# Attention's values by seven block products for eight, in a two-layer decoder trunk on one Trainium2 core

## The chip, the cores and the metric

The kernel runs on one core of one Trainium2 chip. The metric is the device time of one execution in microseconds. The engines of the core are named as in the profile: PE (TensorE), DVE (VectorE), ACT (ScalarE), POOL (GpSimd) and SP (SyncE, which issues most loads).

## The reference

256 tokens of width 2048 go through two layers in float32. Layer 0 has a recurrent mixer, layer 1 has attention; each is followed by an MLP of width 8192.

```python
for layer in range(DEPTH):
    hn = rms_norm(h, norm_mix[layer])
    if layer % 2 == 0:
        mix = recurrent_mixers(hn, ...)
    else:
        mix = dilated_attention(hn, positions, w_qkv[j], w_o[j])
    h = h + mix
    h = h + squared_relu_mlp(rms_norm(h, norm_mlp[layer]), mlp_w1[layer], mlp_w2[layer])
return rms_norm(h, final_norm)

def dilated_attention(h, positions, w_qkv, w_o):
    qkv = (h @ w_qkv).reshape(bsz, seq, 3, ATTN_HEADS, HEAD_DIM)
    q = partial_rope(qkv[:, :, 0], positions) * (HEAD_DIM ** -0.5)
    k = partial_rope(qkv[:, :, 1], positions)
    v = qkv[:, :, 2]
    ...   # softmax over keys inside three dilated windows, merged by their denominators
    return out @ w_o
```

Attention has 16 heads of 128 features; `w_qkv` is 2048 x 6144.

## The kernel before, in words

**Products in float32.** A weight matrix comes from memory in units of 128 x 2048 numbers (1 MB). ACT rounds each to a high part (`hi`, L102), DVE subtracts to get the low part (`lo`, L103); activations are kept split in the same way (`bufa`, `bufb`). A product is three matmuls: high x high, high x low, low x high (`mm`, L181). Units pass through three buffers each of `raw`, `hi` and `lo`; SP issues the loads in one planned order (`units`, `fetch`), and a load waits for its buffer.

**Block products.** The MLP works on pairs of 512 output columns (`blocks`). Of the eight block products of a 2 x 2 by 2 x 2 block matrix over half of the depth, seven do: the units `a`, `t1`, `t2`, `c`, `t3`, `d`, `t4` are single blocks or sums of blocks of the weights, made by DVE (`combine`, L130) and by accumulating loads on POOL (L142, L148). Each is multiplied with one of the sums of activation blocks in `formx` (or `formh`), 12 matmuls of 128x512. The other half of the depth is multiplied plainly: four units `n`, 24 matmuls each. `ORDERS` holds the order of the products. The results pass between PSUM banks by copies (`hold`) and sums (`final`, `u3`). `formx` is filled from the residual's features by `combos` (L597 to L600) and `part_forms` (L593, L594).

**From tokens to features.** After a residual block is complete (`to_x`, L754, or `add_res`, L609), PE transposes it (`turn`, L184), and ACT and DVE write it split into `bufa` (`split_to`, L235, L236). These turns (`to_features`) stand in a list `later`, which `flush` works off after certain products. At the end of the first MLP the blocks come in the order 1, 0, 3, 2; none of them goes to `formx` there.

**Attention.** Values come in four groups of 512 columns (`tokens_group`), each by plain products: 4 units, 96 matmuls of 128x512. A head takes two projections (`project`: 16 matmuls of 128x512 and 16 of 128x256 each), scaling (L421 to L423), the rotary rotation (`rope`, L853 to L856), the score products (L866, L867), mask, maximum, exponential and division (L869 to L877), three transposes (L880), and the product with the values (`mix`, L888, L889), which is split into `bufb` (L232, L233). The order is: values of heads 0 to 3, those heads, values of 4 to 7, those heads, values of 8 to 11, those heads, heads 12 to 15 up to their weights, their values, their mixes. The rotary tables (`rotary`) are asked for behind the first group of values. Then comes the output projection (`out_project`), whose products go through `bufb` in four groups of four heads for each of four column blocks.

A planner fixes the order of instructions on each engine before the run; PE's product matmuls are chained in program order (`chain`), while score products, transposes of scores and mixes are put between them by the planner. `urgent` raises a priority.

Of the kernel before, what the change touches and what calls it, by code (L numbers as in the profile page):

```python
# [20 lines left out]
P = 128  # L21
# [20 lines left out]
def trunk_kernel(ctx, tc, x, xtok, cols, tab, masks, pos, fin, w_in, w_gate, w_out, w_qkv, w_o, w1, w2, out):  # L42
# [81 lines left out]
    def combine(u, src, i, what, i0):  # L124
        def load(name, j, home=wraw):
            held[name] = home.tile([P, 2048], F32, name="raw" if home is wraw else name)
            nc.sync.dma_start(held[name], src[j])

        def add(to, x, y):
            V.tensor_tensor(held[to], held[x], held[y], OP.add)  # L130

        if what == "a":
            load("t1", i0 + 4, pair)
            load("a", i)
            held["s"] = pair.tile([P, 2048], F32, name="s")
# [8 lines left out]
        if ahead == ("t4",) and src not in T4_DMA(w1, w2):  # L144
            add("s", "s", "d")
        made[u] = Weights(held[{"t1": "s", "t2": "s", "t3": "t1", "t4": "s"}.get(what, what)])
        if what == "c" and src in T4_DMA(w1, w2):
            nc.gpsimd.dma_start(held["s"], src[i0 + 1], accum_op=OP.add)  # L148
# [155 lines left out]
    def over_tokens(r):  # L304
        p = psc.tile([P, 512], F32, name="pt", bufs=1)
        for j in range(2):
            T.transpose(p[:, j * P:j * P + P], r[:, j:j + 1].to_broadcast([P, P]), ident)
        return p[:, :S]
# [15 lines left out]
    def tokens(src, i0, mov, kgs=(0, 1, 2, 3), by_k=False):  # L324
        ks = PAIRED if src is w2 else range(KB)
        ps = [pmm.tile([P, 512], F32, name="p") for _ in range(2)]
        for g in kgs:
            w = unit(src, i0 + g)
            order = [(j, i) for i in range(4) for j in range(2)] if by_k else \
                [(j, i) for j in range(2) for i in range(4)]  # L330
            for j, i in order:
                k = ks[4 * g + i]
                h, l = w.part(i * 512, 512)
                xh = mov[:, k, j * P:j * P + P]
                xl = mov[:, k, S + j * P:S + j * P + P]
                first, last = g == kgs[0] and i == 0, g == kgs[-1] and i == 3
                mm(ps[j], xh, h, start=first, stop=False)
                mm(ps[j], xh, l, start=False, stop=False)
                mm(ps[j], xl, h, start=False, stop=last)
            flush()  # L340
        return ps
# [9 lines left out]
    def project(src, i, mov, acc=None):  # L351
        w = unit(src, i)
        p = pmm.tile([P, 512], F32, name="p")
        jobs = [(k, mov[:, k], k == 0, k == KB - 1) for k in range(KB)]
        if later:
            cross(p, w, jobs[:8], "h")
            flush()
            cross(p, w, jobs[8:12], "h")
            cross(p, w, jobs[:12], "l")
            jobs = jobs[12:]  # L360
        (acc or cross)(p, w, jobs)
        return p
# [224 lines left out]
    def open_pairs(layer):  # L587
        pool_ = pairs.enter_context(tc.tile_pool(name=f"pair{layer}", bufs=1))
        return pool_, [pool_.tile([P, 4, 2, 512], F32R, name=n) for n in ("formx", "formh")]
# [12 lines left out]
    pair, (formx, formh) = open_pairs(0)  # L602
# [11 lines left out]
    def to_features(n, gname, forms=None):  # L614
        def work():
            with urgent():
                for half in range(2):
                    p = psc.tile([P, 2, S], F32, name="pl", bufs=2)
                    for j in range(2):
                        for i in range(2):  # L620
                            k = 4 * n + 2 * half + i
                            turn(p[:, i, j * P:j * P + P], xres[:, j, k * P:k * P + P])
                    k = 4 * n + 2 * half
                    if forms is None:
                        for i in range(2):
                            split_to(bufa[:, k + i], p[:, i], col(gname, k + i))
                        continue
                    z = pair.tile([P, 2, 2, P], F32, name="y21")
                    for i in range(2):
                        A.activation(z[:, i], p[:, i].rearrange("p (j c) -> p j c", j=2), AF.Copy,  # L630
                                     scale=col(gname, k + i))
                    zs = z.rearrange("p i j c -> p i (j c)")
                    split_to(bufa[:, k:k + 2], zs)
                    a11, a21, a12, a22 = (z[:, i, j] for i in range(2) for j in range(2))
                    combos(a22, a11, a21, a12, a11, a21, a12, a22)
                    part_forms(forms, k // 2, 1, slice(0, 4), z.rearrange("p i j (one c) -> p one (i j) c", one=1))
        later.append(work)
# [10 lines left out]
    def blocks(src, i0, n0, mov, forms, events, final, soon=False):  # L648
# [6 lines left out]
        beta = psc.tile([P, 512], F32, name="po" if n0 else "pd", bufs=1)  # L655
# [14 lines left out]
        for what, u in ORDERS[src is w2]:  # L670
            w = unit(src, None if u is None else i0 + 4 * n0 + u)
            if what != "n":
# [3 lines left out]
                if what == "t1" and soon:  # L676
                    flush()
                continue
            n, g = divmod(u, 4)
            plains[n] += 1  # L680
            due = len(later)
            for j in (1, 0) if n else (0, 1):
                times(sums[n, j], w, lambda i, j=j, g=g: plain(j, 4 * g + i))
                if plains[n] == 2:
                    final(n, j, sums[n, j])
            flush(due)
# [24 lines left out]
    def first(i0, n0, soon):  # L711
# [23 lines left out]
        def final(n, j, bank):  # L735
            with urgent():
# [5 lines left out]
                else:  # L742
# [5 lines left out]
                                             "t3": u3}, final, soon)  # L748
# [24 lines left out]
    def mlp(layer, nrm, nxt, gname):  # L773
# [13 lines left out]
        for q in range(4):  # L787
            ends = nxt if q == 3 else None

            def done(n):  # L790
                if ends is None:
                    return
                if gname:
                    to_features(n, gname)
# [6 lines left out]
            for n in (0, 2):  # L801
                first(layer * 64 + q * 16, n, q + n == 0)
# [8 lines left out]
    vgs = mixers.enter_context(tc.tile_pool(name="vgs1", bufs=2))  # L811
    wk = mixers.enter_context(tc.tile_pool(name="wk2", bufs=2))
    rot = mixers.enter_context(tc.tile_pool(name="rot", bufs=1))
# [3 lines left out]
    def rotary():  # L817
        ppi = rot.tile([32, S], I32, name="ppi")
        nc.gpsimd.dma_start(ppi, bass.AP(tensor=pos.tensor, offset=pos.offset, ap=[[0, 32], [1, S]]))
        ang = rot.tile([32, S], F32, name="ang")  # L820
        cosT = rot.tile([32, S], F32, name="cosT")
        sinT = rot.tile([32, S], F32, name="sinT")
        V.tensor_copy(ang, ppi)
# [22 lines left out]
    rt = rstd(nx1)  # L846
    rs = tmp.tile([P, S], F32, name="nr", bufs=1)
    A.copy(rs, over_tokens(rt))
# [9 lines left out]
    def scores(u0):  # L858
# [9 lines left out]
        s = wk.tile([P, 384], F32, name="as", bufs=3)  # L868
# [12 lines left out]
        st = wk.tile([P, 384], F32, name="pT", bufs=5)  # L881
# [3 lines left out]
    def mix(hd, st, vg, bank="po", bufs=1):  # L885
        vs = slice((hd % 4) * P, (hd % 4) * P + P)
# [5 lines left out]
    pend = []  # L892
    for g in range(4):
        if g < 3:
            vg = tokens_group(w_qkv, g * 12, rt, kgs=(0, 1, 2, 3) if g else (0, 1, 3, 2))
        if not g:
            rotary()
        for hd in range(4 * g, 4 * g + 4):
            u0 = g * 12 + (4 if g < 3 else 0) + (hd % 4) * 2
            st = scores(u0)  # L900
            if g < 3:
                mix(hd, st, vg)
            else:
                pend.append(st)
    vg = tokens_group(w_qkv, 44, rt)
    for hd, bank in zip(range(12, 16), (("po", 1), ("pd", 1), ("pl", 2), ("pl", 2))):
        mix(hd, pend[hd - 12], vg, *bank)

    mixers.close()
    pair, (formx, formh) = open_pairs(1)  # L910
# [54 lines left out]
T4_DMA = lambda w1, w2: (w1,)  # L965
# [32 lines left out]
def _layout(a):  # L998
# [30 lines left out]
    q_, k_, v_ = feat(wq[:, :2048]), feat(wq[:, 2048:4096]), toks(wq[:, 4096:])  # L1029
    w_qkv = []  # L1030
    for g in range(4):
        if g < 3:
            w_qkv.append(v_[4 * g:4 * g + 4])
        for h in range(4 * g, 4 * g + 4):
            w_qkv += [q_[h:h + 1], k_[h:h + 1]]
    w_qkv.append(v_[12:])
# [33 lines left out]
```

## Time and profile before

| | |
|---|---|
| median of 3 runs | 2166.9 us (2166.84 to 2166.93) |
| the profiled execution's own time | 2166.9 us |
| its span, first to last instruction | 2165.1 us |
| granted PE clock | 0.998 |
| busy PE, DVE, ACT, POOL | 2146.9, 1792.2, 1254.1, 44.7 us |
| first MLP's last quarter | about 931 to 1101 us |
| attention up to the output projection | 1100.7 to 1391.1 us |

A row of groups gives line, engine, operation, output and inputs, shapes and count; then busy time, mean duration in ns, and idle time of the engine before them with what ended it. A row of the timeline gives start, duration, engine, line, and in brackets the idle time before it. A row of stretches gives length, then busy time (and count) of PE, PE's weight loads, DVE, ACT and POOL, then clock, share and rate of the loads. Durations of matmuls are longer than their spacing, since they are pipelined.

### The profile page before, as it was taken

The numbers are of one execution on the slowest core, as the hardware profiler recorded it, in microseconds if no ns is written. First come the engines' busy times: TensorE is split into PE (matmuls) and PEld (weight loads), VectorE is DVE, ScalarE is ACT, GpSimd is POOL, SyncE is SP. The second block draws the span as 40 slices with busy tenths as digits, with TensorE's granted clock in tenths as the row PEclk, the third lists the DMA queues.
The fourth block names the chain that finished last, engine by engine and source line by source line (L and its number), as shares of the span: only waits on it lengthen the run. The fifth ranks groups of instructions, "written<-read, shape, count | busy, mean of one in ns | idle before, by whom it ended". The sixth has DMA issues, their size and how long they took to land.

```text
span 2165.1 us, 27716 instructions
## 1 busy us (share of the span) xinstructions
PE 2146.9 (99%) x11044; PEld 1833.8 (85%) x11044; DVE 1792.2 (83%) x2094; ACT 1254.1 (58%) x1413; POOL 44.7 (2%) x57
## 2 busy tenths in 40 slices
PE   9999999999999999999999999999999999999997
PEld 8999998888888888888788888888888888888886
DVE  7776787789889889889877768667998998898897
ACT  7444485566466566466554544456655755755764
POOL 0000000000000000000000000000000000000000
PEclk9999999999999999999999999999999999999999
DMA  8444445587777687687664554557768777777873
GB/s 319 156 156 164 150 157 212 182 244 246 227 237 257 222 247 235 233 252 233 201 208 166 185 172 161 192 181 227 236 221 261 237 227 238 251 233 224 264 239 129
DMA packets 65857, 464.68 MB, mean 215 GB/s; under 512 B 7344, under 2 KB 8112, under 8 KB 10304
## 3 DMA queue, kind: packets, MB, share of 16 engines
q1 hardware_dynamic: 58176, 410.89, 53.2%
q0 software_dynamic: 7264, 51.42, 12.8%
q8 instruction: 87, 1.43, 0.3%
q10 hardware_dynamic: 288, 0.61, 0.1%
q14 instruction: 42, 0.34, 0.0%
HBM read 460.78 MB, written 2.10 MB: 214 GB/s over the span
## 4 chain that ended last, share of the span: by engine, by line
PE 95%; DVE 2%; ACT 1%; DMA 1%; issue 1%; SPq 0%; DVEq 0%; ACTq 0%
PE p L181 67%; PE po L181 12%; PE pd L181 11%; PE pl L184 2%; DVE lo L103 1%; PE pl L476 1%; ACT hi L102 0%; DMA raw<-in_w 0%; PE pl L867 0%; PE po L888 0%; DVE xall L754 0%; DMA xall<-in_x 0%; PE pd L880 0%; PE pd L460 0%; PE pl L866 0%
## 5 line engine op out<-in xcount | busy, mean ns | idle before, releaser
L102 ACT CAST hi<-raw 128x1024 fp32r<-128x1024 f32 (+2 forms) x486 | 689.3, 1443 | 563.0 <-PE p L181 372.7
L103 DVE TENSOR_TENSOR lo<-raw,hi 128x1024 fp32r<-128x1024 f32 (+2 forms) x486 | 822.2, 1708 | 223.1 <-ACT hi L102 205.4
L181 PE MATMUL p<-hi,bufb 128*128 128x512 f32 x1408 | 448.6, 390 | 2.1 <-DVE xall L754 2.0
L181 PE MATMUL p<-hi,bufa 128*128 128x512 f32 x1280 | 411.4, 392 | 0.8 <-ACT hi L102 0.8
L181 PE MATMUL p<-bufa,hi 128*128 128x256 f32 (+1 forms) x1792 | 364.9, 317 | 0.1
L181 PEld LDWEIGHTS p<-hi,bufb 128*128 128x128 f32 x1408 | 264.3, 188 | 60.1 <-DVE xall L754 5.5
L181 PEld LDWEIGHTS p<-bufa,hi 128*128 128x128 f32 x1792 | 294.5, 190 | 18.9 <-DVE hz L418 0.3
L181 PEld LDWEIGHTS p<-hi,bufa 128*128 128x128 f32 x1280 | 240.4, 188 | 53.0 <-DVE y L718 2.4
L181 PE MATMUL p<-lo,bufb 128*128 128x512 f32 x704 | 274.2, 389 | 1.2 <-DVE lo L103 1.2
L181 PE MATMUL p<-bufa,lo 128*128 128x256 f32 x1152 | 255.5, 287 | 0.0
L181 PE MATMUL p<-lo,bufa 128*128 128x512 f32 x640 | 250.6, 392 | 2.2 <-DVE lo L103 2.1
L103 DVE TENSOR_TENSOR lo<-s,hi 128x2048 fp32r<-128x2048 f32 x96 | 219.4, 2285 | 18.4 <-ACT hi L102 16.5
L102 ACT CAST hi<-s 128x2048 fp32r<-128x2048 f32 x96 | 183.7, 1913 | 48.3 <-PE po L181 21.8
L181 PEld LDWEIGHTS p<-bufa,lo 128*128 128x128 f32 x1152 | 189.3, 191 | 2.6
L181 PEld LDWEIGHTS p<-lo,bufb 128*128 128x128 f32 x704 | 132.2, 188 | 28.4 <-DVE lo L103 1.6
L181 PEld LDWEIGHTS p<-lo,bufa 128*128 128x128 f32 x640 | 120.2, 188 | 28.1 <-DVE lo L103 4.3
L130 DVE TENSOR_TENSOR s<-s,raw 128x2048 f32<-128x2048 f32 x48 | 109.5, 2282 | 1.3 <-DMA raw<-in_w 1.3
L181 PE MATMUL po<-hi,bufa 128*128 128x512 f32 x256 | 84.8, 392 | 0.0
L181 PE MATMUL pd<-hi,bufa 128*128 128x512 f32 x256 | 84.8, 392 | 0.0
L181 PE MATMUL p<-hi,formx 128*128 128x512 f32 x256 | 84.0, 389 | 0.0
L181 PE MATMUL p<-hi,formh 128*128 128x512 f32 x256 | 84.0, 389 | 0.0
L181 PE MATMUL pd<-hi,bufb 128*128 128x512 f32 x256 | 83.0, 389 | 0.0
(281 smaller groups left out, 2754.9 us busy)
## 6 DMA issues: line engine op xcount, KB each, us to landing
raw<-in_w SPq DMA_DIRECT2D x224, 1024.0 KB, 5.1
raw<-in_w_qkv SPq DMA_DIRECT2D x48, 1024.0 KB, 4.8
raw<-in_w_in SPq DMA_DIRECT2D x46, 1024.0 KB, 4.9
t<-in_w SPq DMA_DIRECT2D x32, 1024.0 KB, 5.7
t<-in_w POOLq DMA_DIRECT2D x32, 1024.0 KB, 8.7
raw<-in_w_out SPq DMA_DIRECT2D x16, 1024.0 KB, 4.9
s<-in_w POOLq DMA_DIRECT2D x16, 1024.0 KB, 9.2
raw<-in_w_o SPq DMA_DIRECT2D x16, 1024.0 KB, 4.8
```

What stands on the lines that cost most here:

```text
L102: A.copy(h, w)
L103: V.tensor_tensor(l, w, h.bitcast(F32), OP.subtract)
L130: V.tensor_tensor(held[to], held[x], held[y], OP.add)
L181: chain[:] = [after(T.matmul(*args, **kw), chain)]
L184: chain[:] = [after(T.transpose(out_, in_, ident), chain)]
L476: T.matmul(pl[:, j], kq[:, js], halves(qp[:, js], c, True), start=True, stop=True)
```

## The change

Values come in two pairs of 1024 columns by `blocks`, so with 15/16 of the products (7 for 8 on half of the depth). The banks are summed unscaled, and each result is multiplied by the token's factor `rt` at the end. The pool of `formx`, `s` and `t1` outlives the first MLP (`both`); the first two feature blocks of attention go to `formx` too. The order becomes: first pair of values, heads 0 to 7, heads 8 to 11 up to their weights, second pair, the mixes of 8 to 11, heads 12 to 15. The rotary tables are ordered behind the first pair's last sum on DVE. A turn of features leaves the list `later` for a list of its own, `turns`: it runs two products after it is asked for, one unit after in plain products; its two halves use two tiles.

```diff
     def plan2(src, i):
-        for what, u in ORDERS[src is w2]:
+        for what, u in ORDERS[src is not w1]:
...
-            units.extend((w_qkv, i) for i in (0, 1, 3, 2, *range(4, 48)))
+            for v, heads in ((0, 24), (32, 8)):
+                plan2(w_qkv, v)
+                units.extend((w_qkv, v + 8 + i) for i in range(heads))
...
-    later = []
+    later, turns = [], []
...
+    def turn_some(age=2):
+        for t in turns:
+            t[0] += 1
+        for _ in range(2):
+            if turns and turns[0][0] >= age:
+                turns.pop(0)[1]()
...
     def to_features(n, gname, forms=None):
-        def work():
+        def work(half):
...
-                    z = pair.tile([P, 2, 2, P], F32, name="y21")
+                z = pair.tile([P, 2, 2, P], F32, name="y4" if half else "y21")
...
-        later.append(work)
+        turns.extend([0, lambda half=half: work(half)] for half in range(2))
...
-                to_features(n, gname)
+                to_features(n, gname, formx if n < 2 else None)
...
-        V.tensor_copy(ang, ppi)
+        after(V.tensor_copy(ang, ppi), lastv)
...
+    def values(i0):
+        v = vgs.tile([P, 2, 2, 512], F32, name="vg")
+
+        def hold(n, j, copy):
+            def event(bank):
+                with urgent():
+                    copy(v[:, j, n], bank)
+            return event
+
+        def add(n, j, *args, scale=True):
+            with urgent():
+                lastv[:] = [after(V.tensor_tensor(v[:, j, n], *args), [])]
+                if scale:
+                    A.activation(v[:, j, n], v[:, j, n], AF.Copy, scale=rt[:, j:j + 1])
+
+        def final(n, j, bank):
+            if (n, j) == (0, 1):
+                with urgent():
+                    A.activation(v[:, j, n], bank, AF.Copy, scale=rt[:, j:j + 1])
+            elif (n, j) == (1, 0):
+                add(n, j, bank, v[:, j, n], OP.subtract)
+            else:
+                add(n, j, bank, v[:, j, n], OP.add, scale=not n)
+
+        def u3(bank):
+            add(1, 1, v[:, 1, 1], bank, OP.subtract)
+
+        blocks(w_qkv, i0, 0, bufa, formx,
+               {"a": hold(0, 0, A.copy), "t1": hold(1, 1, V.tensor_copy), "t2": hold(1, 0, A.copy), "t3": u3}, final)
+        return v.rearrange("p j n c -> p j (n c)")
+
+    vg = values(0)
...
+    rotary()
+    for hd in range(8):
+        mix(hd, scores(8 + 2 * hd), vg)
+    pend = [scores(24 + 2 * i) for i in range(4)]
+    vg = values(32)
+    for i, bank in enumerate((("po", 1), ("pd", 1), ("pl", 2), ("pl", 2))):
+        mix(8 + i, pend[i], vg, *bank)
+    for i in range(4):
+        mix(12 + i, scores(40 + 2 * i), vg)
...
-T4_DMA = lambda w1, w2: (w1,)
+T4_DMA = lambda w1, w2, w_qkv: (w1, w_qkv)
```

The second pair's bank `beta` is `pt` in place of `pd`, which the heads' transposes use. Pool sizes of attention's tiles are smaller by one buffer in three places.

More of the change, by code (lines that the diff above doesn't have):

```diff
@@ L132, in combine @@
         if what == "a":
-            load("t1", i0 + 4, pair)
+            load("t1", i0 + 4, both)
             load("a", i)
-            held["s"] = pair.tile([P, 2048], F32, name="s")
+            held["s"] = both.tile([P, 2048], F32, name="s")
             add("s", "a", "t1")
@@ L143, in combine @@
             add("s", "s", "c")
-        if ahead == ("t4",) and src not in T4_DMA(w1, w2):
+        if ahead == ("t4",) and src not in T4_DMA(w1, w2, w_qkv):
             add("s", "s", "d")
         made[u] = Weights(held[{"t1": "s", "t2": "s", "t3": "t1", "t4": "s"}.get(what, what)])
-        if what == "c" and src in T4_DMA(w1, w2):
+        if what == "c" and src in T4_DMA(w1, w2, w_qkv):
             nc.gpsimd.dma_start(held["s"], src[i0 + 1], accum_op=OP.add)
@@ L588, in open_pairs @@
         pool_ = pairs.enter_context(tc.tile_pool(name=f"pair{layer}", bufs=1))
-        return pool_, [pool_.tile([P, 4, 2, 512], F32R, name=n) for n in ("formx", "formh")]
+        return pool_, pool_.tile([P, 4, 2, 512], F32R, name="formh")
     def part_forms(f, k, m, at, src):
@@ L600, in combos @@
         V.tensor_tensor(s4, a12, s2, OP.add)
-    pair, (formx, formh) = open_pairs(0)
+    both = ctx.enter_context(tc.tile_pool(name="both", bufs=1))
+    formx = both.tile([P, 4, 2, 512], F32R, name="formx")
+    pair, formh = open_pairs(0)
     def add_res(ps, n, nrm, scale=None):
@@ L614, in to_features @@
     def to_features(n, gname, forms=None):
-        def work():
+        def work(half):
+            k = 4 * n + 2 * half
             with urgent():
[L617 to L627, printed above, removed]
-                    z = pair.tile([P, 2, 2, P], F32, name="y21")
-                    for i in range(2):
[L630 to L636, printed above, removed]
@@ L637, in to_features @@
-        later.append(work)
+                p = psc.tile([P, 2, S], F32, name="pl", bufs=2)
+                for j in range(2):
+                    for i in range(2):
+                        turn(p[:, i, j * P:j * P + P], xres[:, j, (k + i) * P:(k + i) * P + P])
+                if forms is None:
+                    for i in range(2):
+                        split_to(bufa[:, k + i], p[:, i], col(gname, k + i))
+                    return
+                z = pair.tile([P, 2, 2, P], F32, name="y4" if half else "y21")
@@ new lines, in work @@
+                for i in range(2):
+                    A.activation(z[:, i], p[:, i].rearrange("p (j c) -> p j c", j=2), AF.Copy, scale=col(gname, k + i))
+                split_to(bufa[:, k:k + 2], z.rearrange("p i j c -> p i (j c)"))
+                a11, a21, a12, a22 = (z[:, i, j] for i in range(2) for j in range(2))
+                combos(a22, a11, a21, a12, a11, a21, a12, a22)
+                part_forms(forms, k // 2, 1, slice(0, 4), z.rearrange("p i j (one c) -> p one (i j) c", one=1))
@@ L669, in blocks @@
         plains = [0, 0]
-        for what, u in ORDERS[src is w2]:
+        for what, u in ORDERS[src is not w1]:
             w = unit(src, None if u is None else i0 + 4 * n0 + u)
+            due = len(later)
             if what != "n":
@@ L675, in blocks @@
                     events[what](bank[what])
[L676 to L686, printed above, removed]
+            else:
+                n, g = divmod(u, 4)
+                plains[n] += 1
+                for j in (1, 0) if n else (0, 1):
+                    times(sums[n, j], w, lambda i, j=j, g=g: plain(j, 4 * g + i))
+                    if plains[n] == 2:
+                        final(n, j, sums[n, j])
+                flush(due)
+            turn_some()
     def to_h(n, tiles):
@@ L890, in mix @@
         split_to(bufb[:, hd], po)
[L892 to L902, printed above, removed]
-            else:
-                pend.append(st)
-    vg = tokens_group(w_qkv, 44, rt)
@@ L909, in trunk_kernel @@
+    vg = values(0)
+    rs = tmp.tile([P, S], F32, name="nr", bufs=1)
+    with urgent():
+        A.copy(rs, over_tokens(rt, turn))
+    rotary()
[7 more added lines that the diff above has]
+        mix(12 + i, scores(40 + 2 * i), vg)
     mixers.close()
-    pair, (formx, formh) = open_pairs(1)
+    pair, formh = open_pairs(1)
```

60 lines of the change are left out of this document (23 added, 37 removed).

## The prediction

> **What bounds the kernel now.** I read the page first: the busy table and the chain of work that ended last.
>
> ```profile
> span 2165.1 us, 27716 instructions
> ...
> PE 2146.9 (99%) x11044; PEld 1833.8 (85%) x11044; DVE 1792.2 (83%) x2094; ACT 1254.1 (58%) x1413; POOL 44.7 (2%) x57
> ...
> PE 95%; DVE 2%; ACT 1%; DMA 1%; issue 1%; SPq 0%; DVEq 0%; ACTq 0%
> ```
>
> TensorE is busy nearly throughout and carries 95% of the chain, so a matmul that goes away is worth its own time, if nothing else becomes late. The order of instructions shows where to look: TensorE's order is unchanged up to the last quarter of the first MLP and again from early in the output projection behind attention. In the trace of before that is about 1040 to 1400 us, so I took the table by stretches of 100 us and TensorE's waits between 950 and 1500 us.
>
> ```profile
> 1000.00:1100.00 100.00, 98.12 (x452) 81.01 (x451) 90.61 (x74) 59.81 (x61) 2.27 (x3) 1.00 0.64 208
> 1200.00:1300.00 100.00, 100.00 (x557) 87.13 (x556) 76.63 (x153) 47.27 (x78) 0.00 (x0) 1.00 0.53 179
> 1300.00:1400.00 100.00, 100.00 (x552) 86.95 (x551) 77.73 (x165) 48.78 (x89) 0.00 (x0) 1.00 0.51 172
> ...
> PE p L181 <- DVE lo L103: 1.2, 1, 1.2
> PE p L181 <- DVE xall L754: 0.7, 1, 0.7
> ```
>
> Attention has no TensorE wait at all. The last MLP quarter has two, both for VectorE (1.2 and 0.7 us), where VectorE (third number) is at 90.6%. That is what the change can make worse: it takes work from TensorE and gives work to VectorE, in the one stretch where VectorE is already late.
>
> The profiled execution took 2166.9 us, 1.8 us more than its span, and the median of the runs is 2166.9 us too. I add changes of the span to that.
>
> **Fewer products.** The chain in order of time has a run of 96 matmuls of 128x512:
>
> ```profile
> 1422.03 21.78 PE p L181 x96
> ```
>
> That is 0.2269 us for each. Plain values take 4 groups x 96 = 384 such matmuls. A pair by block products takes seven times 12 for the products of sums or single blocks and four times 24 for the plain ones, 180; two pairs take 360. The order of the changed kernel has exactly 24 fewer 128x512 matmuls and no other change in TensorE's counts. 24 x 0.2269 = **5.45 us less**. I bound it by 5.2 and 5.5 (the matmuls around a product's change may run a little closer or wider). The Trainium skill ("TensorE: Matmul & The Clock Gate", "Back-to-back issue gap") gives 131 ns as the sustained spacing at 512 columns, with which this step would save only an estimated 3.1 us; the row above measures 0.2269 in this kernel, so the trace does not agree.
>
> **Features' combinations.** The first two feature blocks that leave the MLP now also get the sums for the block products. Their price is in the first output projection, where it is done already (VectorE, 360 to 440 us):
>
> ```profile
> L236 DVE SCALAR_TENSOR_TENSOR bufa<-pl,c__83,bufa 128x256 fp32r<-128x256 f32 x8 | 3.5, 477 | 0.3 <-ACT bufa L235 0.3
> L233 DVE TENSOR_TENSOR bufa<-y,bufa 128x512 fp32r<-128x512 f32 x4 | 2.8, 692 | 0.0
> L594 DVE TENSOR_TENSOR formx<-y,formx 128x512 fp32r<-128x512 f32 x4 | 2.8, 688 | 1.4 <-ACT formx L593 1.4
> L597 DVE TENSOR_TENSOR y<-y 128x128 f32<-128x128 f32 x4 | 1.2, 292 | 0.1
> ```
>
> A half block costs 0.69 + 4 x 0.29 + 0.69 = 2.5 us of VectorE in place of 2 x 0.48; four halves add some 6.3 us. They fall between 1043 and 1090 us, and the order puts them between weight splits. This is VectorE and TensorE there, before:
>
> ```profile
> 1057.44 2.29 DVE L130 TENSOR_TENSOR s<-s,raw 128x2048 f32<-128x2048 f32 x1 [1.30 <-DMA raw<-in_w]
> 1059.65 0.74 DVE L754 SCALAR_TENSOR_TENSOR xall<-pd,nm,xall 128x512 f32<-128x512 f32 x1
> 1060.31 2.28 DVE L103 TENSOR_TENSOR lo<-raw,hi 128x2048 fp32r<-128x2048 f32 x1
> 1062.51 0.75 DVE L754 SCALAR_TENSOR_TENSOR xall<-po,nm,xall 128x512 f32<-128x512 f32 x1
> 1063.17 2.28 DVE L103 TENSOR_TENSOR lo<-s,hi 128x2048 fp32r<-128x2048 f32 x1
> 1065.37 0.74 DVE L754 SCALAR_TENSOR_TENSOR xall<-p,nm,xall 128x512 f32<-128x512 f32 x1
> ...
> 1062.64 0.50 PE L181 MATMUL p<-lo,bufb 128*128 128x512 f32 x1 [1.17 <-DVE lo L103]
> 1066.17 0.50 PE L181 MATMUL p<-hi,bufb 128*128 128x512 f32 x1 [0.71 <-DVE xall L754]
> 1069.02 1.03 PE L184 MATMUL pl<-tab__181,xall 128*128 128x128 f32 x8
> 1069.81 0.48 PE L181 MATMUL po<-hi,formh 128*128 128x512 f32 x1
> 1091.68 1.03 PE L184 MATMUL pl<-tab__181,xall 128*128 128x128 f32 x8
> ```
>
> From start to start a 2048 split or sum takes 2.20 us, a residual add 0.66; for a form or feature split I take 0.62 and for a combination 0.3. VectorE has to wait for a weight block (landing at 1057.4) before as after, since the split that frees its buffer is not moved; the combinations queued before that wait are hidden in it. Behind it stand now, ahead of the split that TensorE waits for, one combination and one form split (0.92 us), and another form split ahead of the add that frees the bank: that add ends at 1057.44 + 10.1 = 1067.6 instead of 1066.0. TensorE has meanwhile done the turn of a block (0.79 us, 1069.02 to 1069.81) that it did behind these waits before. It reaches the next product at 1070.6 instead of 1069.8: **0.8 us more** (0 if the loads land early; 1.5 if none of the turn is covered).
>
> **Turns two products late.** The turn of the following block stood at 1091.68, behind a 24-matmul product; now it stands in front of it, at 1091.68 - 5.45 + 0.8 = 1087.0. Its second half reads a residual add which in VectorE's order is the last of 30 instructions since 1057.44: nine splits and sums (19.8), seven adds (4.6), five form or feature splits (3.1), nine combinations (2.7), 30.2 us, so ready at 1087.8. TensorE waits from 1087.2: **0.6 us more** (0 to 1.5). On SP the loads keep their order; only the second pair's first block is asked for early, in front of the first head's weights, and waits for a split that VectorE does before their buffers come free.
>
> The two pairs add four accumulating loads on POOL, like these in the MLP:
>
> ```profile
> s<-in_w POOLq DMA_DIRECT2D x16, 1024.0 KB, 9.2
> ```
>
> From the product that lets one start to the one that reads it lie at least 36 matmuls and mostly 60 to 72 (8.2 to 16 us) here as in the MLP, where no TensorE wait hangs on them: nothing, and 1 us each if a landing is late.
>
> **Rotary tables.** Some 20 small operations move behind the first pair's last add. The first heads' split of weights comes between them, and the third projection needs its bank only 17 us after the pair ends, so I cost this at nothing; without that cover it would be at most their own 6 us.
>
> **Heads in rows of eight and four.** Before, four heads alternate with values. A head in steady state:
>
> ```profile
> 1316.90:1329.67 12.77, 12.77 (x78) 11.30 (x77) 11.23 (x26) 6.35 (x13) 0.00 (x0) 1.00 0.51 163
> ...
> 1318.16 3.82 PE L181 MATMUL p<-bufa,hi 128*128 128x512 f32 x16
> 1321.82 2.08 PE L181 MATMUL p<-bufa,lo 128*128 128x256 f32 x16
> 1323.73 0.39 PE L181 MATMUL p<-bufa,hi 128*128 128x512 f32 x1
> ...
> 1318.36 2.36 DVE L103 TENSOR_TENSOR lo<-raw,hi 128x1024 fp32r<-128x1024 f32 x2 [0.48 <-PE p L181]
> ```
>
> VectorE has 11.2 of 12.8 us and waits for TensorE within each head, so a longer row keeps pace: nothing. A projection takes TensorE 3.66 + 1.91 = 5.57 us from start to start (1318.16 to 1323.73); what is left of 12.77 after two, 1.63, goes to a head's score products, transposes and mix, which I share out as 0.6, 0.3 and 0.7. But the second pair follows heads whose scores are still on VectorE. From the score product of the second head in that row of four, VectorE must do, in its order, 28 instructions until the copy that frees the bank of the second product: three 2048 splits, a 2048 sum, that copy, and 23 of the head's kind.
>
> ```profile
> L103 DVE TENSOR_TENSOR lo<-s,hi 128x2048 fp32r<-128x2048 f32 x96 | 219.4, 2285 | 18.4 <-ACT hi L102 16.5
> ...
> L718 DVE COPY y<-p 128x512 f32<-128x512 f32 x16 | 11.0, 688 | 1.9 <-PE p L181 1.0
> ...
> L869 DVE SCALAR_TENSOR_TENSOR as<-pl,tab__181 128x384 f32<-128x384 f32 x16 | 8.9, 557 | 4.6 <-PE pl L867 4.3
> ...
> L422 DVE TENSOR_TENSOR hz<-p,t 128x256 f32<-128x256 f32 x32 | 13.2, 412 | 0.0
> ```
>
> 4 x 2.20 + 0.69 + 2 x 0.56 + 21 at about 0.35 from start to start (their durations are near L422's, the reciprocal and reductions shorter) = 18.0 us, beginning 0.8 us behind the product. From the score product TensorE needs the bank again after the rest of that projection (0.6 + 1.91), the next one with its score product (5.57 + 0.6), and 36 matmuls and one head's transposes (8.17 + 0.3): 17.2 us. VectorE frees it at 18.8. **Wait 1.6 us**, between 0 (operations 6% shorter) and 3 (an exponential on ScalarE comes late in between).
>
> **The last head.** Before, the four last mixes run early in the output projection. Now the last head's mix stands directly in front of the matmul that reads its result:
>
> ```profile
> 1303.75 0.38 PE L889 MATMUL po<-pT,vg 128*128 128x128 f32 x2
> 1304.30 0.37 ACT L232 CAST bufb<-po 128x256 fp32r<-128x256 f32 x1
> 1304.70 0.42 DVE L233 TENSOR_TENSOR bufb<-po,bufb 128x256 fp32r<-128x256 f32 x1 [0.33 <-ACT bufb L232]
> ```
>
> The cast ends 0.9 us after the mix starts: **0.9 us** (0.6; 1.5 if the low part is late too).
>
> The sum: -5.45 + 0.8 + 0.6 + 1.6 + 0.9 = -1.55 us, so **2165.3 us** (2166.9 - 1.55, rounded).
>
> **The rivals.** (1) Full cover: VectorE overlaps its small operations better than I sum them and the new waits stay below 1.1 us together; then the matmuls' saving shows, -5.45 + 0.4 on average, 2161.8 us. For it: attention shows no wait now, and all four waits are differences of two long sums. Against: VectorE at 90.6% and waiting already. (2) A slower kernel by one mechanism: the first sum of the second pair waits for its weight block. It stands ahead of a head's rotary work in VectorE's order. Its load can start only 4 us before the sum; the load that the 1057.44 row waits for took 9.8 us by the chain:
>
> ```profile
> 1047.55 9.79 DMA raw<-in_w
> ...
> raw<-in_w_qkv SPq DMA_DIRECT2D x48, 1024.0 KB, 4.8
> ```
>
> If it takes over 6 us, every further us is a TensorE wait at the next score product, and the copy above is later by as much: 4 us for each of the two places, 2165.3 + 8 = 2173 us. Against: this stretch moves 172 to 179 GB/s, and loads there take 4.8 us (median, the row above). (3) More waits of the same kind, where I found less than 1 us of slack (the sixth product of the last MLP pair, the alpha copy of the first values pair): 1 to 2 us each, 2168.3 us. (4) The work is not less, if the scheduler moved or kept products: the counted order excludes it.
>
> **How the numbers follow.** Forecast case, waits of 1.1 to 6 us in all: 0.58. Rival 1: 0.25. Rival 3: 0.12. Rival 2: 0.05. What a measurement can tell from no change is about 0.2%, 4.3 us: faster than 2162.6 us is rival 1 (its upper edge, -5.45 + 1.1 = -4.35): 0.25. Slower than 2171.2 is rival 2: 0.05. Within: 0.70. The range leaves out rival 2, half of rival 3 and the fastest of rival 1: 2161.2 (no new wait, and a little of the old ones gone) to 2168.6.
>
> **What would show it.** 24 fewer 128x512 matmuls at 0.227 us; around 1061 to 1070 us waits for the low split and the residual add of 1.5 to 3 us in sum; a wait of the turn near 1087; a wait for the values' copy near the start of the second pair; about 1 us in the fourth product of the output projection. A span under 2160 us, or waits in every head, would prove me wrong.

## The result, and the profile after

| | before | after |
|---|---|---|
| median of the runs | 2167.42 us (22 runs, 2166.78 to 2169.63) | 2164.32 us (22 runs, 2163.66 to 2165.32) |
| profiled execution: span | 2165.1 us | 2162.0 us |

The ratio is 0.9986, with a 95% interval from 0.998 to 0.9992: 3.1 us less, 0.14%. The interval leaves out 1, so the gain is there, though it is inside what the prediction called no change. The time is 1.0 us below the forecast. The busy times of the changed kernel:

```profile
PE 2142.9 (99%) x11020; PEld 1829.1 (85%) x11020; DVE 1819.7 (84%) x2114; ACT 1268.8 (59%) x1415; POOL 48.0 (2%) x61
```

TensorE has 24 instructions less and VectorE 27.5 us more. The stretch from 1000 us (VectorE, third number, from 90.6 to 94.9%) and TensorE's waits from 950 to 1500 us:

```profile
1000.00:1100.00 100.00, 97.80 (x450) 80.66 (x449) 94.86 (x81) 64.39 (x67) 3.14 (x4) 1.00 0.67 214
...
PE p L183 <- DVE xall L754: 1.3, 1, 1.3
PE p L183 <- DVE lo L105: 0.9, 1, 0.9
PE p L183 <- ACT bufb L241: 0.5, 1, 0.5
PE p L183 <- DVE vg L899: 0.3, 1, 0.3
```

Three of the four places where the prediction summed a wait show here; the fourth, the turn near 1087, shows only as a longer turn (below). None of its rivals' waits is there. A wait of this view is only the time in which TensorE had nothing in flight, and it costs more than that. Around the 0.25 us for `vg` (rows under number 4) a matmul starts 0.64 us behind the one before it, at 1301.27 for 1300.63, and the next one 0.34 us later, where matmuls of this size start 0.23 us apart: 0.52 us are lost. In the same way the 1.34 us for `xall` cost 1.61, and the two waits of the kernel before 1.44 for 1.17 and 0.98 for 0.71. So some 0.27 us come on top of each, and so I measured between starts. The chain in order of time gives three marks that every kernel here has: the last run of 36 matmuls into `p` before the MLP's last VectorE stretch, the first product of the values, and the first turn in the output projection behind attention. Before:

```profile
1027.70 8.18 PE p L181 x36
...
1100.90 5.44 PE p L181 x24
...
1421.15 0.88 PE pl L184 x8
```

After:

```profile
1027.87 8.17 PE p L183 x36
...
1101.55 2.72 PE pd L183 x12
...
1417.72 0.87 PE pl L186 x8
```

The first stretch (end of the MLP) went from 73.20 to 73.68 us, +0.48. Attention went from 320.25 to 316.17, -4.08. The piece ahead of the marks is 0.17 longer, the piece behind them 0.33 (2165.1 - 1421.15 = 743.95; 2162.0 - 1417.72 = 744.28). Those two are not the change: the order of instructions is the same there, and with that order the last piece is 743.92 us in experiment 1 below and 744.01 in experiment 4. The first mark itself lies between 1027.48 and 1028.83 us in the kernels below that have the same order ahead of it, so spans differ by a microsecond without any edit; the stretches agree far closer.

### The profile page after: what moved, and what is told of

Read it like the earlier page. It is cut to its first block, busy times and chain, and to the rows that moved or that the text cites. A ratio compares the mean times of both kernels' runs of the same rounds, so it can differ in the third digit from the quotient of the medians.

```text
span 2162.0 us, 27706 instructions
## 1 busy us (share of the span) xinstructions
PE 2142.9 (99%) x11020; PEld 1829.1 (85%) x11020; DVE 1819.7 (84%) x2114; ACT 1268.8 (59%) x1415; POOL 48.0 (2%) x61
## 4 chain that ended last, share of the span: by engine, by line
PE 94%; DVE 3%; ACT 1%; DMA 1%; issue 1%; SPq 0%; DVEq 0%; ACTq 0%
PE p L183 65%; PE pd L183 12%; PE po L183 12%; PE pl L186 2%; DVE lo L105 1%; PE pl L479 1%; PE pt L183 1%; ACT hi L104 1%; DMA raw<-in_w 0%; DMA xall<-in_x 0%; PE pl L863 0%; PE po L884 0%; DVE xall L754 0%; PE pd L876 0%; PE pd L463 0%
## 5 line engine op out<-in xcount | busy, mean ns | idle before, releaser
L104 ACT CAST hi<-raw 128x2048 fp32r<-128x2048 f32 (+2 forms) x468 | 684.0, 1484 | 556.2 <-PE p L183 342.6
L105 DVE TENSOR_TENSOR lo<-raw,hi 128x2048 fp32r<-128x2048 f32 (+2 forms) x468 | 816.5, 1759 | 192.2 <-ACT hi L104 176.4
L183 PE MATMUL p<-hi,bufa 128*128 128x512 f32 x1136 | 365.8, 391 | 1.0 <-ACT hi L104 0.7
L183 PEld LDWEIGHTS p<-hi,bufa 128*128 128x128 f32 x1136 | 213.2, 188 | 48.3 <-DVE y L718 2.4
L105 DVE TENSOR_TENSOR lo<-s,hi 128x2048 fp32r<-128x2048 f32 x102 | 233.2, 2286 | 19.0 <-ACT hi L104 17.0
L104 ACT CAST hi<-s 128x2048 fp32r<-128x2048 f32 x102 | 195.2, 1914 | 52.9 <-PE po L183 22.4
L183 PE MATMUL p<-lo,bufa 128*128 128x512 f32 x568 | 221.9, 391 | 1.9 <-DVE lo L105 1.9
L183 PEld LDWEIGHTS p<-lo,bufa 128*128 128x128 f32 x568 | 106.7, 188 | 25.5 <-DVE lo L105 4.1
L183 PE MATMUL p<-hi,formx 128*128 128x512 f32 x288 | 94.9, 390 | 0.0
L105 DVE TENSOR_TENSOR lo<-t,hi 128x2048 fp32r<-128x2048 f32 x34 | 77.8, 2288 | 13.0 <-ACT hi L104 13.0
```

The source lines that it names most:

```text
L104: A.copy(h, w)
L105: V.tensor_tensor(l, w, h.bitcast(F32), OP.subtract)
L183: chain[:] = [after(T.matmul(*args, **kw), chain)]
```

## Experiments

Each is an edit of the changed kernel, except number 5. The two stretches are read from the chain as above; the median is of 11 runs, beside 33 of the kernel before on the same chip. Number 2 leaves out work: its block products of the values read the forms of an earlier layer, so only its time counts.

| | MLP's end, us | attention, us | median, us | ratio to before, 95% |
|---|---|---|---|---|
| before | 73.20 | 320.25 | | |
| after | 73.68 | 316.17 | 2164.32 | 0.9986 (0.998 to 0.9992) |
| 1 both pairs plain | 73.73 | 321.02 | 2168.77 | 1.0008 (0.9999 to 1.0017) |
| 2 no forms for the mixing layer | 72.16 | 316.14 | 2162.05 | 0.9977 (0.9968 to 0.9986) |
| 3 last reader later | 73.86 | 315.87 | 2164.10 | 0.9985 (0.9976 to 0.9994) |
| 4 bank by ScalarE | 73.64 | 315.66 | 2163.82 | 0.9985 (0.9977 to 0.9994) |
| 5 late turns alone | 72.29 | 320.25 | 2166.84 | 0.9997 (0.9988 to 1.0006) |
| 6 mix ahead | 73.79 | 315.12 | 2163.29 | 0.9982 (0.9973 to 0.999) |
| 7 three late | 71.95 | 318.07 | 2167.65 | 1.0001 (0.9992 to 1.0009) |
| 8 combinations on GpSimd | 75.91 | 316.28 | 2166.10 | 0.9994 (0.9986 to 1.0003) |
| 9 mix ahead, bank by ScalarE | 73.80 | 314.63 | 2162.69 | 0.9979 (0.997 to 0.9988) |
| 10 as 9, forms asked for a product later | 73.79 | 314.64 | 2162.79 | 0.9979 (0.997 to 0.9987) |
| 11 tables unordered | 73.88 | 316.15 | 2163.77 | 0.9984 (0.9975 to 0.9993) |
| 12 second pair plain | 73.81 | 318.31 | 2166.30 | 0.9995 (0.9987 to 1.0004) |

Stretches that an edit doesn't touch agree within some 0.2 us, so a stretch tells about a quarter of a microsecond, ten times finer than the ratios.

### What the products are worth: 1 and 12

```diff
-    vg = values(0)
+    vg = plain_values(0)      # eight products of 24 matmuls
...
-    vg = values(32)
+    vg = plain_values(32)     # number 12: this one alone
```

`plain_values` gives each group of 512 columns its own two banks, four products of 24 matmuls, and scales by `rt` in ScalarE's copy, as the kernel before did.

> Both values pairs by eight plain products (384 matmuls for 360), everything else of the change kept: the order 8+4+4 heads, the forms of the features, the turns two products late, the tables behind pair one. Theory (the gain is the 24 matmuls, less 0.4 to 0.6 us that the second pair loses on the bank that VectorE frees): the span grows by 5.45 - 0.5 = 4.9 us, from 2162.0 to 2166.9, about 1.8 us over the kernel before; the wait for the copy of line 899 is gone, the waits around 1057 to 1089 stay. Rival (the new order of the work brings time by itself): it grows by less than 3.1 us and stays under the 2165.1 of the kernel before. Rival (the pairs' sums cost more than 0.5): it grows by less than 4.

> Only the second values pair by eight plain products (12 matmuls more). Theory (each pair saves 12 x 0.227 = 2.72, and the second gives 0.7 of it back at the bank): 2.0 us slower than the changed kernel, span 2164.0; with both plain it was 4.3 to 4.5, so the first pair alone is worth 2.3 to 2.7. Rival (the second pair saves nothing net, since its weight sums hold VectorE up among the heads): 2162.0.

```profile
1101.36 5.44 PE p L183 x24
...
1422.38 0.87 PE pl L186 x8
```

With both pairs plain, attention takes 321.02 us, 4.85 more than with block products (forecast 4.9), and the median is 1.8 us over the kernel before (2168.77 against 2166.97; the interval just touches 1). With the second pair plain it takes 318.31, 2.14 more (forecast 2.0): the second pair is worth 2.14, and the first 321.02 - 318.31 = 2.71, which is 12 x 0.2269 = 2.72. The gain is the 24 matmuls, all of the first twelve and most of the second. The new order of rows brings little by itself: plain values in it take 0.77 us more than in the old order, less than the 1.05 that its last head costs (number 6).

### What the forms cost, and what the late turns give: 2 and 5

```diff
-                    to_features(n, gname, formx if n < 2 else None)
+                    to_features(n, gname)
```

> Left out: the combinations and form splits of the feature blocks 0 to 7 in the last quarter of the first MLP, so the block products of the values read the forms of an earlier layer. Turns, splits and matmuls stay, two products late. Theory (this VectorE work delays a weight split and a residual add that TensorE waits for): 0.5 us goes, the span is 2161.5. Rival (the forms cost what the prediction summed, 0.8 + 0.6): 1.4 us goes, 2160.6. Rival (the late turns cost it, not the forms): no change, 2162.0.

Number 5 puts `turns`, `turn_some` and the halved `to_features` into the kernel before, in place of `later` there.

> The kernel before with one part of the change: feature blocks turned in halves, two products late (one in the output projections); values by plain products in four groups, rotary tables and head rows as before, no forms for the mixing layer. Theory (leaving the forms out of the changed kernel took 1.5 us from the stretch 1057 to 1089, but the changed kernel is only 0.5 later there than the kernel before; so the late turns give back about 1.0): the span is 2164.1, 1.0 under the kernel before, and the waits there are those of the run without forms. Rival (late turns do nothing by themselves; the 1.0 comes with the values' order): 2165.1.

The chain's marks and TensorE's waits from 1030 to 1100 us, number 2:

```profile
1028.18 8.18 PE p L183 x36
...
1100.34 2.72 PE pd L183 x12
...
PE p L183 <- DVE xall L754: 0.7, 1, 0.7
```

Number 5:

```profile
1028.37 8.18 PE p L181 x36
...
1100.66 5.44 PE p L181 x24
...
PE p L181 <- DVE lo L103: 0.3, 1, 0.3
```

Without the forms the stretch is 72.16: they cost 1.52 us, near the 1.4 of the first rival and not the 0.5 of the theory. The late turns alone take the kernel before from 73.20 to 72.29: they give 0.91 (forecast 1.0). There the wait for the low split is 0.3 us where it was 1.2, since the turn of 0.87 us now stands in front of it and covers it. The two numbers together make the +0.48 of the whole change to 0.13 us. Number 5's gain is too small for the medians: 0.5 us, its interval goes past 1.

### The second pair's bank: 4

```diff
-               {"a": hold(0, 0, A.copy), "t1": hold(1, 1, V.tensor_copy), "t2": hold(1, 0, A.copy), "t3": u3}, final)
+               {"a": hold(0, 0, A.copy), "t1": hold(1, 1, A.copy if i0 else V.tensor_copy), "t2": hold(1, 0, A.copy), "t3": u3}, final)
```

> In the second values pair ScalarE for VectorE copies the second product out of its bank. Theory (the 0.4 us of start-to-start delay at 1301.3 is VectorE's queue): the wait for the copy goes and 0.4 to 0.6 us with it, the span is 2161.5. Rival (ScalarE's own queue with casts of 1.9 us is as late): the wait stands on line 899 again, by ScalarE, and the span is 2162.0 to 2162.8.

In the changed kernel VectorE copies the bank, and TensorE waits for it:

```profile
1297.88 0.39 PE L183 MATMUL p<-hi,formx 128*128 128x512 f32 x1
...
1300.54 0.67 DVE L899 COPY vg<-p 128x512 f32<-128x512 f32 x1
...
1300.63 0.39 PE L183 MATMUL p<-hi,bufa 128*128 128x512 f32 x1
1301.27 0.50 PE L183 MATMUL p<-hi,bufa 128*128 128x512 f32 x1 [0.25 <-DVE vg L899]
1301.61 0.40 PE L183 MATMUL p<-lo,bufa 128*128 128x512 f32 x1
```

The product that it copies has its last matmul at 1297.88, so the copy starts 2.3 us behind that one's end (1298.27). With ScalarE it is 0.5 us (the end is 1298.76 there), and the wait is gone:

```profile
1298.37 0.39 PE L183 MATMUL p<-hi,formx 128*128 128x512 f32 x1
...
1299.25 0.58 ACT L899 COPY vg<-p 128x512 f32<-128x512 f32 x1
```

Attention is 0.51 us shorter, as forecast (0.4 to 0.6) and as the starts around the wait say (0.52). ScalarE's casts of 1.9 us were not in the way; the planner put the copy ahead of one.

### The last head's mix: 3 and 6

Number 3 changes the order of the reader alone, number 6 also places the mix.

```diff
-            add_res(tokens(src, 4 * n, bufb, kgs), n, nrm)
+            add_res(tokens(src, 4 * n, bufb, kgs, src is w_o and not n), n, nrm)   # number 3
...
+    st = scores(46)                                                               # number 6
+    ps0 = tokens(w_o, 0, bufb, by_k=True, at_six=lambda: mix(15, st, vg, put=mm))
```

> In the first group of the output projection behind attention the two token halves alternate by feature block, so the first matmul that reads the last head comes 9 matmuls (2.0 us) later. Theory (the planner puts the last mix directly in front of its reader, whatever its input's time): the mix moves along, TensorE still loses about 0.9 us from start to start there, the span stays 2162.0. Rival (the mix is placed when its input is ready, 1404.9, and the reader comes too early): the loss goes, 2161.1.

> The mix of the last head is put by hand into the first group of the output projection, 12 matmuls ahead of the first matmul that reads it (its input has been there since 1404.9 in the changed kernel), and that group alternates the token halves. Theory (0.9 us is lost because the mix stands directly in front of its reader): the loss goes, the span is 2161.1 or a little less, and the wait for line 241's bufb is gone. Rival (ScalarE's weight casts of 1 us stand ahead of the cast that the reader needs): 0.4 of it stays, 2161.6. Rival (no change, as when only the reader was later): 2162.0.

The changed kernel, at the mix:

```profile
1406.99 0.59 PE L884 MATMUL po<-pT,vg 128*128 128x256 f32 x2
...
1407.84 0.37 ACT L241 CAST bufb<-po 128x256 fp32r<-128x256 f32 x1 [0.68 <-PE po L885]
1408.27 0.49 PE L183 MATMUL p<-hi,bufb 128*128 128x512 f32 x1 [0.46 <-ACT bufb L241]
1408.60 0.40 PE L183 MATMUL p<-lo,bufb 128*128 128x512 f32 x1
1409.00 0.74 PE L183 MATMUL p<-hi,bufb 128*128 128x512 f32 x2
...
1408.53 0.42 DVE L242 TENSOR_TENSOR bufb<-po,bufb 128x256 fp32r<-128x256 f32 x1
```

The same place in number 3:

```profile
1410.19 0.59 PE L884 MATMUL po<-pT,vg 128*128 128x256 f32 x2
...
1411.04 0.37 ACT L241 CAST bufb<-po 128x256 fp32r<-128x256 f32 x1 [2.72 <-PE po L885]
...
1411.80 0.40 PE L183 MATMUL p<-lo,bufb 128*128 128x512 f32 x1
1412.04 0.62 PE L183 MATMUL p<-hi,bufb 128*128 128x512 f32 x2
...
1411.44 0.42 DVE L242 TENSOR_TENSOR bufb<-po,bufb 128x256 fp32r<-128x256 f32 x1 [1.68 <-ACT bufb L241]
```

The reader went 9 matmuls back and the mix went with it: the same chain of mix, cast and reader, and a gain of 0.30 us for 0.9. The gain is the low part, which VectorE writes behind the cast and which the reader's third matmul needs. In the changed kernel VectorE is still at a weight split and starts it 0.69 us behind the cast's start; in number 3 it is free and starts it after 0.40. The reader and the four matmuls behind it take 1.54 us in the changed kernel (1408.27 to 1409.81) and 1.25 in number 3 (1411.47 to 1412.72). In number 6 the mix is in TensorE's order by hand, ahead of twelve matmuls (it stands under line 183 then, as everything that `mm` issues):

```profile
1406.09 0.81 PE L183 MATMUL po<-pT,vg 128*128 128x256 f32 x4
1406.66 0.48 PE L183 MATMUL p<-hi,bufb 128*128 128x512 f32 x1
1406.94 0.37 ACT L241 CAST bufb<-po 128x256 fp32r<-128x256 f32 x1
```

No wait follows, and attention is 1.05 us shorter. So the loss is the mix's place directly in front of its reader: from the mix to the next product it is 0.57 us here and 1.28 in the changed kernel, 0.71 more, and the late low part makes 0.29.

### The forms at another time or on another engine: 7, 8 and 10

```diff
-    def turn_some(age=2):
+    def turn_some(age=3):                                          # number 7
...
-                combos(a22, a11, a21, a12, a11, a21, a12, a22)
+                combos(a22, a11, a21, a12, a11, a21, a12, a22, nc.gpsimd if gname == "nmix1" else V)   # number 8
...
+            formed.append(made_forms) if gname == "nmix1" else made_forms()   # number 10
```

> Feature blocks turned three products late for two. Theory (the forms cost VectorE time wherever they stand, and what they delay is a weight split and a residual add): within 0.5 us of the changed kernel, span 2161.5 to 2162.5. Rival (one more product lets the late transfer of 1057 pass first): 1.0 or more goes, 2161.0 or less. Rival (the turned blocks are now needed sooner than they are ready): slower by 1 us or more, 2163 or more.

> The four combinations of each half of the mixing layer's feature blocks 0 to 7 (16 subtractions and additions of 128x128 in all) run on GpSimd, the forms' split stays on VectorE. Theory (what costs 1.5 us is VectorE's time on the forms; 16 x 0.2 of 16 x 0.2 + 4 x 0.7 = 6.0 us is taken away): half of it goes, the span is 2161.3. Rival (GpSimd's operations hold up VectorE's or the accumulating loads that GpSimd issues): no gain or a loss, 2162.0 to 2164.

> As e9, and the combinations and form splits of the mixing layer's blocks are issued one product after the turn they belong to. Theory (the forms' 6 us of VectorE cost 1.5 because they stand in front of a weight split and a residual add; moved, they stand in front of others as long as VectorE is 95% busy in this stretch): within 0.6 us of e9, 2159.7 to 2160.9. Rival (only their place behind the late transfer of 1057 costs): 1.0 or more goes, 2159.3 or less.

Number 7 came out as its last rival said: it brought a wait that the changed kernel doesn't have, in three places:

```profile
PE p L183 <- DVE bufa L245: 4.1, 3, 1.4
```

One more product of delay takes 1.73 us from the MLP's end, and the wait for the bank there is gone. But the turned blocks now come too late for the products that read them, behind both output projections and in the values (+1.90 in attention). Three products late only for the blocks that are not needed at once was not tried.

Number 8 made the stretch 2.23 us longer, as its rival said. GpSimd, VectorE and ScalarE at the place:

```profile
1050.05 2.53 DVE L105 TENSOR_TENSOR lo<-raw,hi 128x2048 fp32r<-128x2048 f32 x1 [0.90 <-ACT hi L104]
1050.39 2.51 POOL L602 TENSOR_TENSOR y<-y 128x128 f32<-128x128 f32 x1
1055.35 0.45 POOL L603 TENSOR_TENSOR y<-y 128x128 f32<-128x128 f32 x1
1070.04 5.25 POOL L600 TENSOR_TENSOR y<-y 128x128 f32<-128x128 f32 x1 [13.27 <-DVE bufa L242]
1079.58 0.62 ACT L596 CAST formx<-y 128x512 fp32r<-128x512 f32 x1 [4.63 <-POOL y L603]
```

An operation takes 0.45 us there when VectorE is between instructions, 2.51 when a split of 2048 columns is under way, and 5.25 over a sum and a split; the splits beside it take up to 2.53 instead of 2.29. So the combinations come late and hold the forms up: ScalarE's cast of a form waits 4.63 us for the last of them, and its weight casts stand behind that cast. Number 10 says nothing of another time (73.79 against 73.80). From 1000 to 1110 us VectorE and ScalarE run their instructions in the order of the changed kernel, one for one; the first form split stands behind the same residual add, at 1060.16 for 1060.45. The planner put the forms where they had been, so whether they would cost as much elsewhere stays open.

### Tables without their place: 11

```diff
-        after(V.tensor_copy(ang, ppi), lastv)
+        V.tensor_copy(ang, ppi)
```

> The rotary tables without the dependence on the last addition of the first values pair: the planner spreads their 16 VectorE operations over the end of the first MLP and the first pair, where VectorE is 87 to 95% busy. Theory (behind pair one they cost nothing; here each of about 0.15 to 0.4 us delays what waits for VectorE): 0.5 to 1.5 us slower, 2162.5 to 2163.5. Rival (they fall into VectorE's gaps, the order is worth nothing): 2162.0.

My theory was wrong: 73.88 and 316.15 us are the changed kernel's numbers within the spread. The tables run from 1095 to 1126 us, at the MLP's end and among the first pair's work, and bring no new wait of TensorE, so putting them behind the pair neither costs nor brings anything.

### Two edits together: 9

> Two edits on the changed kernel together: the last head's mix 12 matmuls ahead of its reader (alone 1.0 us from matmul start to matmul start) and the second pair's bank copied out by ScalarE (alone 0.7). Theory (two waits 100 us apart that have nothing in common): they add up to 1.7, the span is 2160.3 and the median 1.7 under the changed kernel's 2164.3. Rival (the time won at the bank is waited out again in front of the output projection's weights): 1.0, as with the mix alone.

Attention takes 314.63 us, 1.54 less than in the changed kernel; alone the two edits brought 1.05 and 0.51, so they add up as the theory said. The median of 2162.69 us is the lowest here of a kernel that does the whole work: 4.7 us under the kernel before in the same runs.

## Why the prediction was right, and where its sizes were off

The sum was -5.45 + 0.8 + 0.6 + 1.6 + 0.9 = -1.55 us; -3.1 was measured, and -3.60 in the two stretches alone. The parts and the signs were right, the four waits made 2.04 us for 3.9, and two of them were too large by half a microsecond or more. That the time came out only 1.0 us off is luck in part: the median of the kernel before is 0.5 us higher in these runs than in the three that the forecast started from, and another 0.5 us lies outside the stretches.

**Fewer products**, -5.45: right. The first pair alone measured 2.71 of 2.72.

**Features' combinations**, +0.8: 0.41 measured. The first product behind the waits starts 42.52 us behind the first mark, before 42.11:

```profile
1063.40 0.50 PE L183 MATMUL p<-lo,bufb 128*128 128x512 f32 x1 [0.87 <-DVE lo L105]
...
1066.72 0.75 DVE L754 SCALAR_TENSOR_TENSOR xall<-p,nm,xall 128x512 f32<-128x512 f32 x1
...
1067.52 0.50 PE L183 MATMUL p<-hi,bufb 128*128 128x512 f32 x1 [1.34 <-DVE xall L754]
...
1070.39 0.39 PE L183 MATMUL po<-hi,formh 128*128 128x512 f32 x1
```

VectorE's sum held: one combination and one form split stand in front of the low split and another form split in front of the add, as foreseen, and the add ends 10.09 us behind the row at 1057.38 that the load releases, summed as 10.1. What was off lies at both ends: against the first mark the load comes 0.23 us earlier than before (1057.38 - 1027.87 = 29.51 for 29.74), and from the add to the next product it takes 2.92 us where 3.0 were allowed. The 1.52 us for all forms in number 2 and the 0.91 that the turn covers in number 5 are the two sides that this step put together.

**Turns two products late**, +0.6: 0.07 measured, the largest error in proportion. The turn's row is 0.15 us longer than one without a wait:

```profile
1081.92 0.29 DVE L602 TENSOR_TENSOR y<-y 128x128 f32<-128x128 f32 x1
1082.12 0.29 DVE L603 TENSOR_TENSOR y<-y 128x128 f32<-128x128 f32 x1
...
1086.23 0.74 DVE L754 SCALAR_TENSOR_TENSOR xall<-po,r2n,xall 128x512 f32<-128x512 f32 x1
1086.72 1.18 PE L186 MATMUL pl<-tab__181,xall 128*128 128x128 f32 x8
```

The mis-sized quantity is the combination: 0.3 us each were summed, nine times, from the duration in the first output projection. Here two halves' combinations alternate, no two neighbours depend on each other, and they start 0.20 apart. That is 0.9 us too much. The add ended 29.59 us behind the row at 1057.38, where 30.2 were summed; a gap of 0.2 us in front of the split at 1083.42 took a part back. The end of the sum was also misread: 1057.44 + 30.2 is 1087.6 and not 1087.8, so by its own numbers the wait was 0.4 us.

**The second pair's wait**, +1.6: 0.51 measured in number 4. VectorE's side was right again in total: 18.86 us from the score product at 1282.35 to the end of the copy at 1301.21, summed as 18.8. TensorE's side was not 17.2 but 18.5, from the score product to 1300.86, where the next matmul would have started without a wait:

```profile
1282.35 0.38 PE L862 MATMUL pl<-hz 128*128 128x128 f32 x2
...
1282.82 1.50 PE L183 MATMUL p<-bufa,hi 128*128 128x512 f32 x5
...
1286.07 3.82 PE L183 MATMUL p<-bufa,hi 128*128 128x512 f32 x16
```

The prediction let 2.5 us of that projection be left behind the score product; from the product to the next projection it was 3.72. Not only the low part's matmuls were left, but five of the sixteen high ones too (the row at 1282.82). A difference of two sums of 18 us each was wrong by the error of one of them.

**The last head**, +0.9: 1.05 measured, as what number 6 took away; the waits' table (0.46) shows only half of it. The size is right in part by luck. The forecast's 0.9 ran from the mix's second half to the end of the cast, without taking off the mix's own time; what that chain costs is 0.71. The late low part, kept for the upper bound, makes up the other 0.29.

**Rotary tables, longer rows, loads**, 0: right. The attention stretch leaves -4.08 + 5.45 - 0.51 - 1.05 = -0.19 us to all else.

**Rivals.** Full cover did not come: 2.0 us of the forecast's waits are there (0.41 + 0.07 + 0.51 + 1.05). The slow rival began and stayed without effect: the second pair's first sum did wait for its block, 0.81 us, and no TensorE wait hangs on it.

```profile
1268.89 2.29 DVE L132 TENSOR_TENSOR s<-raw,t 128x2048 f32<-128x2048 f32 x1 [0.81 <-DMA raw<-in_w_qkv]
```

## What to carry to other kernels

Where one engine is busy throughout, the saving of a block product can be counted from its instructions, and what is left to predict is which new waits the extra additions bring. Measure such a wait from start to start of the matmuls around it and between marks that both kernels have: that tells a quarter of a microsecond where medians tell one or two. An operation that a planner places directly in front of its reader goes along when the reader moves; put it into the engine's order yourself. After an edit that should move something, look in the trace whether the order moved at all (number 10).

## What the runs showed of the hardware

GpSimd and VectorE held each other up: an operation of 128x128 took 0.45 us on GpSimd alone, 2.51 and 5.25 beside VectorE's 2048-column operations, and of these one took 2.53 instead of 2.29. The Trainium skill says of this, in "SBUF — State Buffer", section "SBUF: two separate sides", that the two share a pair of ports by an exclusive lock for a whole instruction, which a VectorE operation with two SBUF inputs takes as well. The trace agrees: a blocked operation lasts about as long as what VectorE does beside it.

Independent operations of 128x128 on VectorE last 0.29 us and start 0.20 apart, so the sum of a row of them by their durations is nearly half too large. In the first output projection, where each works on what its neighbour reads or writes, they last as long and start 0.33 apart (367.84, 368.17, 368.49 and 368.82 us in the kernel before).

A wait of TensorE in a stream of 128x512 matmuls cost its idle time and some 0.27 us more: 0.52 for 0.25, 0.98 for 0.71, 1.44 for 1.17 and 1.61 for 1.34. One directly behind a turn cost 1.23 for 0.87.
